# Row scaling beside items 4 to 11, and raw weight blocks and background weights in two spare half buffers

## The chip, the cores and the metric

The program runs on one core of a Trainium2 chip. The metric is device time in microseconds (us) of one execution; lower is better. Three executions of the kernel before took 2995.53, 2995.94 and 2998.75 us, a median of 2995.94. The profile is that of a further execution, which took 2992.3 us in all and 2990.3 us from its first instruction to its last.

## The reference

The model is a trunk of two layers over one sequence of 1024 rows with 1024 channels, all in float32. Layer 0 mixes with a gated delta rule, layer 1 with retention; each is followed by a projection, a residual with layer norm, and a gated feed-forward network (FFN) with a short convolution. A conditioning vector gives each layer scales, shifts and gates ("ada").

```
# layer 1's mixer
q, k, v, gate = split(h @ w_in)            # 4 heads; q, k: 256 channels, v, gate: 512 per head
q, k = rope(q), rope(k)
o = chunked retention over 8 chunks of 128 rows (state S per head)
o = layer-norm-like per head (no affine) of o, times silu(gate)
out = o @ w_out
# after each mixer
x = layer_norm(ALPHA * x + (1 + ada_gate) * out) * g + b
```

The gate row "1 + ada_gate" of layer 1's retention is `silu(c) @ ada_w[1][:, 2*1024:3*1024] + ada_b`: a vector times a 1024 x 1024 block. The kernel computes it on VectorE (DVE), a weight row block at a time, in the background of other work.

## The kernel before, in words

Matmuls are float32-accurate: every operand is split into a high and a low part (fp32r), and three matmuls of 128x512 make one product (`mm3`, L110 to L112; `L1138` and `L616` for other callers). TensorE (PE) therefore does almost all of the span. The split of a block is one copy on ScalarE (ACT, L89, the high part) and one subtraction on DVE (L90, the low part).

The instructions are recorded in program order and then ordered by a scheduler which models the time of each; buffers are tiles with a fixed number per tag ("wr": two of 128x1024, "xT": two of 128x512, "auh", "lane" and so on). A tile's load waits until the last reader of the tile before it in the same buffer is done. Loads are issued by SyncE (SP), one queue, in its order; a DMA in front that waits holds up the ones behind it. So the tag of a load sets when it can start.

Places that the change touches:

- **The opening** (to about 70 us) uses the two "xT" buffers for transposed input (L517). After that they are unused for the rest of the kernel.
- **Layer 1's q, k and gate stage** (about 1430 to 1790 us): a Strassen-Winograd scheme over 16 items, `strassen(..., direct=True, beside=scale_rows)`. Items 0 and 1 are done plainly by `side`; items 2 to 15 by `wino(n)`: two raw weight blocks of 128x1024 are loaded (`ua` by L1190, `ub` by L1191, both tag "wr"), sums s1 to s4 of their halves are made on DVE (L1184, `psub`), split (L89, L90), and seven products of twelve matmuls each are made. Items 2, 4, 5, 7, 9, 11, 12 and 14 are q or k blocks: their outputs go through a rotation on DVE (L1614 to L1619, 12 instructions of 128x512), and are stored by GpSimd (POOL) to `qd` (L1620). The others are gate blocks, which end on ACT (L1629).
- **scale_rows(n)** is called by `wino(n)`. Before, it does for each of items 8 to 15 two blocks of 128x512 of the residual rows: SP loads `xg` (L1646), POOL multiplies by the layer norm's gain and adds its bias (L1647, L1648), and POOL stores the block (L1649).
- **The transition** (about 1775 to 1800 us): SP loads `xlo`, the rows from which the other half of the transposed input is made (PE L259); `qk` from `qd` (L1806); and `wr<-in_ret_wv` (L102), the raw weights of v.
- **The core** (about 1790 to 2150 us): a stream `ret_fill` makes v (`ret_v`, L616; its weights go through both "wr" buffers, each then split by ACT L89 into `wh` and by DVE L90 into `wl`), and runs interleaved with the streams `core(h)` of the four heads: state update Sr (DVE L1739, L1741), output, its normalisation `on` (DVE L1761 to L1767), the product with the gate `ot` (L1776).
- **The background weights of the core**: `bg_ada(1, 2, "row")` gives 16 steps. A step loads 128x2x512 `mvw` (L210, tag `bg_tag[0]`, which is "wr" there) and does two DVE instructions (L214 for the first, then L216: `ada = mvw * e + ada`). Eight such instructions make a half of the vector (four steps of L210 each); then PE sums over partitions (L238) and DVE adds it to the row (L239). Two halves are made.

Of the kernel before, what the change touches and what calls it, by code (L numbers as in the profile page):

```python
# [12 lines left out]
ALU = mybir.AluOpType  # L13
AX = mybir.AxisListType

P = 128
D = 1024
S = 1024
KT = D // P
HALF = 512  # L20
# [13 lines left out]
def trunk_kernel(ctx: ExitStack, tc, A):  # L34
# [166 lines left out]
    def bg_ada(i, j, kind):  # L201
        box = {}

        def unit(nh, kp):
            if kp == 0:
                box["a"] = tl("ada", [P, HALF])
            a = box["a"]
            wr = tl(bg_tag[0], [P, 2, HALF], name="mvw")
            c0 = j * D + nh * HALF
            sp.dma_start(wr, A["ada_w"][i, kp * 256:(kp + 1) * 256, c0:c0 + HALF].rearrange("(a p) n -> p a n", p=P))  # L210
            for kk in range(2):
                k = kp * 2 + kk
                if k == 0:
                    dve.tensor_scalar(a, wr[:, 0], e[:, 0:1], None, ALU.mult)  # L214
                else:
                    dve.scalar_tensor_tensor(a, wr[:, kk], e[:, k:k + 1], a, ALU.mult, ALU.add)  # L216
            if kp < KT // 2 - 1:
                return
            if kind == "col":
                if nh == 0:  # L220
                    vecs[i, j] = ct(f"v{i}{j}", [P, KT])
                gs = slice(4 * nh, 4 * nh + 4)
                v, b = vecs[i, j][:, gs], bias_cols(i, j)[:, gs]
                tp, pt = bg_ps[0](), tl("sm2", [P, 4], name="cs")
                for g in range(4):
                    pe.transpose(tp[:, g * P:(g + 1) * P], a[:, g * P:(g + 1) * P], ident)
                for g in range(4):
                    act.activation(a[:, g * P:(g + 1) * P], tp[:, g * P:(g + 1) * P], AF.Copy, accum_out=pt[:, g:g + 1])
                if j in (1, 2, 4):
                    dve.scalar_tensor_tensor(v, pt, 1.0, b, ALU.add, ALU.add)  # L230
                else:
                    dve.tensor_add(v, pt, b)
            else:
                if nh == 0:
                    rows[i, j] = row_load(A["ada_b"][i:i + 1, j * D:(j + 1) * D], ("x", i))
                g = rows[i, j][nh]
                pt = bg_ps[0]()
                pe.matmul(pt, ones, a, start=True, stop=True)  # L238
                dve.scalar_tensor_tensor(g, pt, 1.0, g, ALU.add, ALU.add)  # L239

        for nh in range(2):
            for kp in range(KT // 2):
                bg.append(lambda nh=nh, kp=kp: unit(nh, kp))
# [888 lines left out]
    def strassen(hT0, xts, scale, shift, items, tags=("hTb", "hTb", "qkv", "qkv", "aux"), direct=False, beside=None):  # L1132
# [53 lines left out]

        def wino(n, sink):
            ua, ub = items[n][:2]
            wa, wb = tl("wr", [P, D]), tl("wr", [P, D])
            sp.dma_start(wa, ua)  # L1190
            anchor["i"] = sp.dma_start(wb, ub)  # L1191
            if beside:
                beside(n)
            a11, a12, a21, a22 = wa[:, hs(0)], wa[:, hs(1)], wb[:, hs(0)], wb[:, hs(1)]
            def copy_of(X, tag="cv"):
                t = tl(tag, [P, 516] if tag == "cv" else [P, HALF], name="pc")[:, 0:HALF]
                act.activation(t, X, AF.Copy)  # L1197
                return t

            X = prod(a11, "11")  # L1200
            p1 = copy_of(X)
            s1 = psub(a21, a22, ALU.add)
            sink(0, prod(a12, "21"), p1)
            s2 = psub(s1, a11)
            Z = prod(s1, "T1")
            z5 = copy_of(Z)
            s4 = psub(a12, s2)
            prod(s2, "T2", X)
            u2 = copy_of(X)
            s3 = psub(a11, a21)  # L1210
            prod(s4, "22", Z)
            sink(1, Z, u2)
            bg_step()
            prod(s3, "T3", X)
            u3 = copy_of(X, "t2")
            sink(3, X, z5)
            sink(2, prod(a22, "T4"), u3)
            bg_step()
# [416 lines left out]
    gb = []  # L1635

    def scale_rows(n):
        for u in range(2 * (n - 8), 2 * (n - 8) + 2) if n >= 8 else ():
            c, rs = u // 8, slice(u % 8 * P, u % 8 * P + P)
            if u % 8 == 0:  # L1640
                gb[:] = [tl("auh", [P, HALF], name="gb") for _ in range(2)]
                for t, nm in zip(gb, ("ln_g", "ln_b")):
                    sp.dma_start(t, A[nm][1:2, hs(c)].to_broadcast([P, HALF]))
            x = tl("auh", [P, HALF], name="xg")
            with after("i"):
                sp.dma_start(x, xs[1][rs, hs(c)])  # L1646
            pool.tensor_tensor(x, x, gb[0], ALU.mult)  # L1647
            pool.tensor_tensor(x, x, gb[1], ALU.add)  # L1648
            pool.dma_start(xg[0][rs, hs(c)], x)  # L1649
# [175 lines left out]
            yield r  # L1825

    mix = []
    events["core", -1] = clk[0]
    free["qkv"] = 20
    run([(0.0, ret_fill())] + [(-1.0, core(h)) for h in range(RH)])  # L1830
    layer_tail(1, mix, None, xs[1], xs[2], A["out"], None, True)


# [100 lines left out]
```

## Time and profile before

| what | value |
|---|---|
| median of three executions | 2995.94 us (2995.53 to 2998.75) |
| the profiled execution | 2992.3 us, span 2990.3 us |
| mean granted TensorE clock | 0.980 |
| PE busy | 2827.8 us, 95% of the span |
| DVE busy | 2191.9 us, 73% |
| ACT busy | 1347.4 us, 45% |
| POOL busy | 604.6 us, 20% |
| L216 (`ada<-mvw,e,ada`), all of the kernel | 140 instructions, 107.1 us, 27.2 us of DVE's idle time before them |

How to read it. PE is busy for 95% of the span, so time can be won or lost only where PE stands idle, and where its granted clock is below 1: after an idle time of some microseconds PE runs at half clock for a while. DVE is not the engine with the most work, yet an instruction of PE often waits for one on DVE, and DVE runs its instructions in a fixed order: one that waits for a DMA holds up all behind it. "[2.40 <-DVE wb L90]" behind a row means that the engine had been idle for 2.40 us, and that the wait ended with an instruction of DVE at line 90 which writes a tile named wb.

### The profile page before, as it was taken

What the parts mean: (1) busy time and instruction counts of PE and PEld (TensorE: products, weight loads), DVE (VectorE), ACT (ScalarE), POOL (GpSimd) and SP (SyncE); (2) the same over time, 40 slices, a digit from 0 to 9 for tenths busy, and PEclk for the clock granted to TensorE, in tenths of its full rate; (3) what the DMA queues carried; (4) which work ended last, traced back from release to release, by engine and by line L of the source; (5) the groups of instructions that cost most, each with busy time, mean ns of one, the idle gap of its engine ahead of it and who ended that gap; (6) DMA issues with size and microseconds to landing.
All of it is one profiled execution on the core that took longest, in us unless ns stands there. A gap on an engine that the chain in (4) does not pass through costs nothing.

```text
span 2990.3 us, 38893 instructions
## 1 busy us (share of the span) xinstructions
PE 2827.8 (95%) x13638; PEld 2308.4 (77%) x13638; DVE 2191.9 (73%) x3877; ACT 1347.4 (45%) x2513; POOL 604.6 (20%) x629
## 2 busy tenths in 40 slices
PE   8889998999999999999999989989999899999996
PEld 7768877887778888877787777767778688888785
DVE  5785687545588888997677665656687787778888
ACT  4655555434544444536443333212345544445444
POOL 0411221133011111520002330232201011112603
PEclk9999999999999999999999999999999999999998
DMA  7222221344344444864424453556573333335652
GB/s 273 86 77 72 96 89 64 117 159 137 110 141 162 155 151 147 311 204 135 154 79 145 157 210 119 170 169 183 169 248 125 127 134 106 106 106 200 242 179 106
DMA packets 235379, 442.35 MB, mean 148 GB/s; under 512 B 22192, under 2 KB 75696, under 8 KB 235184
## 3 DMA queue, kind: packets, MB, share of 16 engines
q1 hardware_dynamic: 205024, 387.96, 38.9%
q10 hardware_dynamic: 25152, 34.61, 3.2%
q0 software_dynamic: 5008, 17.30, 1.5%
q8 instruction: 107, 1.75, 0.2%
q14 instruction: 88, 0.72, 0.1%
HBM read 331.26 MB, written 108.53 MB: 147 GB/s over the span
## 4 chain that ended last, share of the span: by engine, by line
PE 68%; DVE 13%; issue 8%; DMA 6%; ACT 4%; POOL 2%; SPq 0%; POOLq 0%; ACTq 0%; DVEq 0%
PE acc L616 15%; PE acc L1412 11%; PE acc L1138 8%; PE acc L110 5%; PE acc L111 4%; PE acc L112 4%; PE sc L616 4%; PE sc L1138 3%; PE sc L1412 3%; PE mm L616 2%; PE sc L111 2%; PE sc L110 2%; PE sc L112 2%; DMA mvw<-in_ada_w 1%; DVE qkv L435 1%
## 5 line engine op out<-in xcount | busy, mean ns | idle before, releaser
L1412 PE MATMUL acc<-bb,ab 128*128 128x512 f32 x1800 | 427.7, 392 | 3.7 <-DVE bb L90 1.5
L1412 PEld LDWEIGHTS acc<-bb,ab 128*128 128x128 f32 x1800 | 337.3, 188 | 78.2 <-DVE bb L90 3.9
L616 PE MATMUL acc<-hT,wh 128*128 128x512 f32 x960 | 301.2, 395 | 0.0
L1548 POOL TENSOR_TENSOR o<-o 128x512 f32<-128x512 f32 x88 | 118.3, 1354 | 719.5 <-DVE o L1541 684.7
L1138 PE MATMUL acc<-T,wb 128*128 128x512 f32 x840 | 209.4, 400 | 12.6 <-DVE wb L90 12.6
L616 PEld LDWEIGHTS acc<-hT,wh 128*128 128x128 f32 x960 | 183.4, 191 | 33.8
L616 PE MATMUL acc<-hT,wl 128*128 128x512 f32 x480 | 203.5, 424 | 0.2 <-ACT sg L1064 0.2
L89 ACT ACTIVATE ab<-ar 128x512 fp32r<-128x512 f32 x210 | 129.4, 624 | 158.7 <-PE acc L1412 85.6
L1138 PEld LDWEIGHTS acc<-T,wb 128*128 128x128 f32 x840 | 161.2, 193 | 50.6 <-DVE wb L90 16.9
L90 DVE TENSOR_TENSOR ab<-ar,ab 128x512 fp32r<-128x512 f32 x210 | 172.9, 830 | 30.1 <-ACT ab L89 29.7
L90 DVE TENSOR_TENSOR wb<-wr,wb 128x512 fp32r<-128x512 f32 x162 | 114.2, 710 | 86.8 <-ACT wb L89 86.5
L90 DVE TENSOR_TENSOR wl<-wr,wh 128x1024 fp32r<-128x1024 f32 x85 | 104.2, 1225 | 97.3 <-ACT wh L89 97.3
L89 ACT ACTIVATE wh<-wr 128x1024 fp32r<-128x1024 f32 x101 | 106.8, 1058 | 129.9 <-PE acc L616 61.5
L90 DVE TENSOR_TENSOR wb<-mm,wb 128x512 fp32r<-128x512 f32 x216 | 145.1, 685 | 21.1 <-ACT wb L89 19.1
L1197 ACT ACTIVATE pc<-acc 128x512 f32<-128x512 f32 x143 | 84.6, 592 | 160.9 <-PE acc L1138 108.2
L89 ACT ACTIVATE wb<-mm 128x512 fp32r<-128x512 f32 x216 | 122.4, 593 | 76.5 <-DVE mm L1184 76.2
L89 ACT ACTIVATE wb<-wr 128x512 fp32r<-128x512 f32 x162 | 98.9, 626 | 98.8 <-DMA wr<-in_ffn_up 49.5
L616 PE MATMUL acc<-wh,hT 128*128 128x512 f32 x384 | 137.1, 420 | 2.5 <-DVE vv L90 1.6
L1527 DVE SCALAR_TENSOR_TENSOR o<-g,vc,o 128x512 f32<-128x512 f32 (+2 forms) x176 | 135.3, 787 | 0.9 <-ACT o L1522 0.2
L435 DVE SCALAR_TENSOR_TENSOR qkv<-raw,vc,qkv 128x512 f32<-128x512 f32 x144 | 114.8, 801 | 26.8 <-ACT qkv L433 25.5
L216 DVE SCALAR_TENSOR_TENSOR ada<-mvw,e,ada 128x512 f32<-128x512 f32 x140 | 107.1, 765 | 27.2 <-DMA mvw<-in_ada_w 27.1
L110 PE MATMUL acc<-T,wb 128*128 128x512 f32 x292 | 116.7, 400 | 9.9 <-DVE wb L90 9.4
(620 smaller groups left out, 7079.8 us busy)
## 6 DMA issues: line engine op xcount, KB each, us to landing
wr<-in_ffn_up SPq DMA_DIRECT2D x96, 512.0 KB, 4.4
mvw<-in_ada_w SPq DMA_DIRECT2D x80, 512.0 KB, 4.4
ad<-o SPq DMA_DIRECT2D x154, 256.0 KB, 2.3
ar<-ad SPq DMA_DIRECT2D x154, 256.0 KB, 4.0
Br<-in_ffn_down SPq DMA_DIRECT2D x66, 256.0 KB, 3.8
wr<-in_ret_wv SPq DMA_DIRECT2D x32, 512.0 KB, 3.9
ar<-od SPq DMA_DIRECT2D x56, 256.0 KB, 5.2
xs<-xt ACTq DMA_DIRECT2D x24, 512.0 KB, 3.1
```

What stands on the lines that cost most here:

```text
L89: act.activation(dst_h, src, AF.Copy)
L90: eng.tensor_tensor(dst_l, src, dst_h, ALU.subtract)
L110: mm(acc, wl[:, k], hl[0], start=first, stop=False)
L111: mm(acc, wh[:, k], hl[1], start=False, stop=False)
L112: mm(acc, wh[:, k], hl[0], start=False, stop=last)
L216: dve.scalar_tensor_tensor(a, wr[:, kk], e[:, k:k + 1], a, ALU.mult, ALU.add)
L435: dve.scalar_tensor_tensor(oh, raw[:, 3 - j:515 - j], w[:, 3 - j:4 - j], oh, ALU.mult, ALU.add)
L616: pq(pe.matmul(out, lhsT, rhs, start=start, stop=stop, **kw), cost)
L1138: return pe.matmul(*a, skip_group_check=True, **kw)
L1412: mm_ = (lambda *a, p=p, onto=onto, **kw: (mm if p < 2 else pe.matmul)(*a, skip_group_check=onto, **kw))
L1527: dve.scalar_tensor_tensor(tv, gv[:, c0 - j:c1 - j], w[:, 2 - j:3 - j], tv, ALU.mult, ALU.add)
L1548: pool.tensor_tensor(o[d], o[x], o[y], op)
```

## The change

Three things are changed.

1. `scale_rows` does its two blocks beside items 4 to 11 and not beside items 8 to 15. The work is the same.
2. In the q, k and gate stage the raw weight blocks of `wino` are numbered m = 2n (`ua`) and 2n + 1 (`ub`). Every third one (m = 6, 9, ... 30, nine blocks) is loaded as two halves of 128x512 into the two "xT" buffers; the others go through the two "wr" buffers as before. So three raw blocks can be held and not two.
3. During the core `bg_tag` is "xT": a step of the background weights is loaded as two halves of 128x512 into the two "xT" buffers, by two DMAs of 256 KB in place of one of 512 KB. Both "wr" buffers are left to the weights of v.

The numbers of instructions on PE, ACT, DVE and POOL stay as they are; SP issues 17 DMAs more (1184 before, 1201 now).

```diff
@@ bg_ada
-            wr = tl(bg_tag[0], [P, 2, HALF], name="mvw")
             c0 = j * D + nh * HALF
-            sp.dma_start(wr, A["ada_w"][i, kp * 256:(kp + 1) * 256, c0:c0 + HALF].rearrange("(a p) n -> p a n", p=P))
+            src = A["ada_w"][i, kp * 256:(kp + 1) * 256, c0:c0 + HALF].rearrange("(a p) n -> p a n", p=P)
+            if bg_tag[0] == "xT":
+                wr = [tl("xT", [P, HALF], name="mvw") for _ in range(2)]
+                for a2 in range(2):
+                    sp.dma_start(wr[a2], src[:, a2])
+            else:
+                wt = tl(bg_tag[0], [P, 2, HALF], name="mvw")
+                sp.dma_start(wt, src)
+                wr = [wt[:, 0], wt[:, 1]]
             for kk in range(2):
                 k = kp * 2 + kk
                 if k == 0:
-                    dve.tensor_scalar(a, wr[:, 0], e[:, 0:1], None, ALU.mult)
+                    dve.tensor_scalar(a, wr[0], e[:, 0:1], None, ALU.mult)
                 else:
-                    dve.scalar_tensor_tensor(a, wr[:, kk], e[:, k:k + 1], a, ALU.mult, ALU.add)
+                    dve.scalar_tensor_tensor(a, wr[kk], e[:, k:k + 1], a, ALU.mult, ALU.add)
@@ wino
-            wa, wb = tl("wr", [P, D]), tl("wr", [P, D])
-            sp.dma_start(wa, ua)
-            anchor["i"] = sp.dma_start(wb, ub)
+            raws = []
+            for m, u in ((2 * n, ua), (2 * n + 1, ub)):
+                if direct and m % 3 == 0:
+                    raws += [tl("xT", [P, HALF], name="wr") for _ in range(2)]
+                    for h2 in range(2):
+                        anchor["i"] = sp.dma_start(raws[-2 + h2], u[:, hs(h2)])
+                else:
+                    w = tl("wr", [P, D])
+                    anchor["i"] = sp.dma_start(w, u)
+                    raws += [w[:, hs(0)], w[:, hs(1)]]
             if beside:
                 beside(n)
-            a11, a12, a21, a22 = wa[:, hs(0)], wa[:, hs(1)], wb[:, hs(0)], wb[:, hs(1)]
+            a11, a12, a21, a22 = raws
@@ scale_rows
-        for u in range(2 * (n - 8), 2 * (n - 8) + 2) if n >= 8 else ():
+        for u in range(2 * (n - 4), 2 * (n - 4) + 2) if 4 <= n < 12 else ():
@@ the core
+    bg_tag[0] = "xT"
     events["core", -1] = clk[0]
     free["qkv"] = 20
     run([(0.0, ret_fill())] + [(-1.0, core(h)) for h in range(RH)])
+    bg_tag[0] = "wr"
```

The scheduler's order moves with it. Line numbers of the changed kernel are higher: L1184 becomes L1191, L1190 and L1191 become L1201 (half blocks) and L1204, L210 becomes L213 (half blocks), L214 and L216 become L221 and L223, lines from 1214 on become higher by 14.

**SP at the end of the q, k and gate stage.** Before, in a row (`xg` are the rows to be scaled, `qk` the rotated blocks, `xlo` the rows to be transposed, `wr<-in_ret_wv` v's weights):

```order
L1646 DMA xg<-xs_67 128x512 x2
L1190 DMA wr<-in_ret_wg 128x1024
L1191 DMA wr<-in_ret_wg 128x1024
L1646 DMA xg<-xs_67 128x512 x2
L1806 DMA qk<-qd 128x512 x2
L1665 DMA xlo<-xs_67 128x512 x2
L1806 DMA qk<-qd 128x512 x10
L102 DMA wr<-in_ret_wv 128x1024
L1665 DMA xlo<-xs_67 128x512 x2
L102 DMA wr<-in_ret_wv 128x1024
```

Now, at the same place (`mvw` are the background weights):

```order
L1204 DMA wr<-in_ret_wg 128x1024
L102 DMA wr<-in_ret_wv 128x1024
L1679 DMA xlo<-xs_67 128x512 x2
L1820 DMA qk<-qd 128x512 x2
L213 DMA mvw<-in_ada_w 128x512
L1820 DMA qk<-qd 128x512 x7
L1679 DMA xlo<-xs_67 128x512 x2
L102 DMA wr<-in_ret_wv 128x1024
L1785 DMA gt<-gd 128x4x128
L1820 DMA qk<-qd 128x512 x3
L213 DMA mvw<-in_ada_w 128x512 x2
L102 DMA wr<-in_ret_wv 128x1024 x2
```

The `xg` loads are gone from here, v's first weights stand ahead of the `qk` loads, four of the `qk` loads stand earlier still, and the first background weights are loaded here and not in the middle of the core.

**DVE at the transition.** Before, from the last sums of item 15 (`hT` and `wl` are splits for v):

```order
L1129 TENSOR_TENSOR pc<-sc,pc 128x512 x2
L90 TENSOR_TENSOR wl<-wr,wh 128x1024
L90 TENSOR_TENSOR hT<-t_15335,hT 128x512
L90 TENSOR_TENSOR hT<-t_15345,hT 128x512
L90 TENSOR_TENSOR wl<-wr,wh 128x1024
L90 TENSOR_TENSOR hT<-t_15355,hT 128x512
L90 TENSOR_TENSOR hT<-t_15365,hT 128x512
L90 TENSOR_TENSOR wl<-wr,wh 128x1024 x2
```

Now:

```order
L223 SCALAR_TENSOR_TENSOR ada<-mvw,e,ada 128x512
L90 TENSOR_TENSOR hT<-t_15353,hT 128x512
L90 TENSOR_TENSOR hT<-t_15363,hT 128x512
L223 SCALAR_TENSOR_TENSOR ada<-mvw,e,ada 128x512
L90 TENSOR_TENSOR wl<-wr,wh 128x1024
L90 TENSOR_TENSOR hT<-t_15373,hT 128x512
L223 SCALAR_TENSOR_TENSOR ada<-mvw,e,ada 128x512
L90 TENSOR_TENSOR hT<-t_15383,hT 128x512
L223 SCALAR_TENSOR_TENSOR ada<-mvw,e,ada 128x512
L90 TENSOR_TENSOR wl<-wr,wh 128x1024
L223 SCALAR_TENSOR_TENSOR ada<-mvw,e,ada 128x512 x3
L90 TENSOR_TENSOR wl<-wr,wh 128x1024
```

All eight background instructions of the vector's first half now stand here (the first, L221, inside the rotation of item 14), where before they stood in the core between 1960.9 and 2003 us. The last three stand ahead of the split of the fifth weight block of v.

**DVE in the core, at the second half of the background vector.** Before (the first row is the first background instruction, the last `on` is the one whose time the prediction speaks of):

```order
L214 TENSOR_SCALAR ada<-mvw,e 128x512
L1741 SCALAR_TENSOR_TENSOR Sr<-Sr,sc 128x512
L216 SCALAR_TENSOR_TENSOR ada<-mvw,e,ada 128x512
L1741 SCALAR_TENSOR_TENSOR Sr<-Sr,sc 128x512
L1776 TENSOR_TENSOR ot<-mm,gt 128x512
L216 SCALAR_TENSOR_TENSOR ada<-mvw,e,ada 128x512
L1704 SCALAR_TENSOR_TENSOR kz<-mm,vc,kz 128x256
L1706 TENSOR_TENSOR sT<-mm,dx 128x128
L216 SCALAR_TENSOR_TENSOR ada<-mvw,e,ada 128x512
L90 TENSOR_TENSOR sThl<-sT,sThl 128x128
L1761 BN_STATS rst<-sc 128x6
L1763 BN_AGGR mv<-rst 128x2
```

Now, from behind the sT of that piece on:

```order
L223 SCALAR_TENSOR_TENSOR ada<-mvw,e,ada 128x512 x2
L90 TENSOR_TENSOR sThl<-sT,sThl 128x128
L1775 BN_STATS rst<-sc 128x6
L1777 BN_AGGR mv<-rst 128x2
L223 SCALAR_TENSOR_TENSOR ada<-mvw,e,ada 128x512
L1778 TENSOR_SCALAR mv<-mv 128x1
L90 TENSOR_TENSOR wl<-wr,wh 128x1024
L223 SCALAR_TENSOR_TENSOR ada<-mvw,e,ada 128x512
L1781 TENSOR_SCALAR on<-sc,mv 128x512
L1755 SCALAR_TENSOR_TENSOR Sr<-Sr,sc 128x512
L223 SCALAR_TENSOR_TENSOR ada<-mvw,e,ada 128x512
```

Before, four of the eight background instructions stand ahead of the `on` that follows this piece, and four behind it; now six stand ahead of it (the L221 and the first L223 as in the piece before, and the four in this one) and two behind. They are fed by a ring of two half blocks.

## The prediction, made blind

> **What bounds the kernel now.** I read the page's head first, then PE, clock and DMA by stretches of the stage that the change touches, then what PE waited for there.
>
> ```profile
> PE 2827.8 (95%) x13638; PEld 2308.4 (77%) x13638; DVE 2191.9 (73%) x3877; ACT 1347.4 (45%) x2513; POOL 604.6 (20%) x629
> PE 68%; DVE 13%; issue 8%; DMA 6%; ACT 4%; POOL 2%; SPq 0%; POOLq 0%; ACTq 0%; DVEq 0%
> ```
>
> PE is the bound, so only its idle time and its clock can be won. The stretches (columns: busy time and instructions of each engine, granted clock, DMA share, GB/s):
>
> ```profile
> 1440.00:1460.00 20.00, 20.00 (x91) 16.55 (x90) 15.08 (x38) 7.92 (x20) 2.19 (x4) 1.00 0.42 158
> 1660.00:1680.00 20.00, 17.60 (x71) 14.13 (x70) 16.20 (x26) 6.87 (x13) 5.68 (x6) 0.91 0.46 170
> 1720.00:1740.00 20.00, 16.65 (x66) 13.33 (x66) 16.81 (x26) 5.71 (x10) 8.88 (x8) 0.91 0.33 119
> 1780.00:1800.00 20.00, 16.44 (x64) 12.48 (x63) 5.63 (x7) 6.64 (x10) 0.91 (x2) 0.83 0.97 350
> 2000.00:2050.00 50.00, 44.35 (x189) 33.76 (x190) 36.14 (x69) 10.14 (x18) 6.19 (x13) 0.93 0.51 159
> ```
>
> Where nothing waits (1440), PE is busy throughout at full clock. In the others it idles and the clock drops: the missing clock costs 20 x 0.09 = 1.8 us in each of the first two, 20 x 0.17 = 3.4 us at 1780, 50 x 0.07 = 3.5 us at 2000. What PE waited for, by groups of 1427 to 1790 us (last column) and by single rows (in brackets the idle time and who ended it):
>
> ```profile
> L1138 PE MATMUL acc<-T,wb 128*128 128x512 f32 x216 | 55.6, 409 | 7.5 <-DVE wb L90 7.5
> L1138 PE MATMUL sc<-T,wb 128*128 128x512 f32 x120 | 29.4, 394 | 4.0 <-DVE wb L90 4.0
> 1530.70 0.50 PE L1138 MATMUL sc<-T,wb 128*128 128x512 f32 x1 [0.61 <-DVE wb L90]
> 1590.08 0.73 PE L1138 MATMUL sc<-T,wb 128*128 128x512 f32 x2 [1.06 <-DVE wb L90]
> 1670.46 3.86 PE L1138 MATMUL acc<-T,wb 128*128 128x512 f32 x9 [2.40 <-DVE wb L90]
> 1734.22 0.74 PE L1138 MATMUL acc<-T,wb 128*128 128x512 f32 x2 [3.35 <-DVE wb L90]
> 1789.83 0.69 PE L259 MATMUL mm<-cst,xlo 128*128 128x128 f32 x2 [2.70 <-DMA xlo<-xs]
> 1791.34 0.79 PE L616 MATMUL acc<-wh,hT 128*128 128x512 f32 x1 [0.82 <-ACT wh L89]
> 2003.93 1.65 PE L616 MATMUL sc<-vv,sThl 128*128 128x512 f32 x3 [4.96 <-DVE Sr L1739]
> ```
>
> So four places: the rotations (11.5 us idle + 3.6 of clock), the transition (2.70 + 0.82 + 3.4 = 6.9), the core's first background half (4.96 + 3.5, and small gaps), and its second half.
>
> **The rotations: -5 us.** There are eight gaps, one behind each q or k item, since DVE's split of the next block is queued behind the rotation. Two things make them long:
>
> ```profile
> L1616 DVE TENSOR_TENSOR rm<-pc,sinT 128x512 f32<-128x512 f32 x16 | 16.4, 1025 | 0.0
> L1617 DVE TENSOR_TENSOR pc<-pc,cosT 128x512 f32<-128x512 f32 x16 | 14.9, 930 | 0.2
> L1618 DVE TENSOR_TENSOR rm<-rm,pc 128x512 f32<-128x512 f32 x16 | 11.0, 685 | 0.0
> 1658.52 1.78 DVE L1616 TENSOR_TENSOR rm<-pc,sinT 128x512 f32<-128x512 f32 x1
> 1656.76 2.99 POOL L1647 TENSOR_TENSOR xg<-xg,gb 128x512 f32<-128x512 f32 x2 [11.21 <-DMA xg<-xs]
> 1656.04 0.70 DVE L1184 TENSOR_TENSOR mm<-wr 128x512 f32<-128x512 f32 x1 [2.43 <-DMA wr<-in_ret_wg]
> DVE mm L1184 <- DMA wr<-in_ret_wg: 5.9, 5, 2.4
> DVE mm L1184 <- DMA wr<-in_ret_wqk: 1.8, 2, 1.0
> ```
>
> First, the same DVE operation takes 685 ns alone and up to 1.78 us beside POOL's scaling; over the two slowed lines that is 16 x (1025 - 685) + 16 x (930 - 685) ns = 9.4 us. [...] Second, DVE stands 7.7 us (5.9 + 1.8) before a weight block that lands late; 2.43 of it just ahead of the rotation at 1658, whose gap is 2.40. With a third buffer the block's load is issued one block earlier, so I take these waits as gone. The scaling is not: of the eight rotations (items 2, 4, 5, 7, 9, 11, 12, 14) items 9, 11, 12 and 14 are in its range before, and 4, 5, 7, 9 and 11 now. That speaks against the change: one more rotation is exposed. But the worst gap is that of 12, close behind 11, and there the scaling leaves; its twin is 5, close behind 4 (1.06 without scaling). I take 0.6 for 2 and 14, 1.1 for 4, 7, 9, 11 and 12, 2.2 for 5 (between 1.06 and 3.35): 8.9, and one clock drop in two cases, 0.9. That is 15.1 - 9.8, say -5. Bounds: all gaps at 0.61 (-10); the same pairs at the old price in items 4 and 5 and one more exposed gap of 1.2 (+1).
>
> [...] Here a gap of 2.40 already brings the slice to 0.91, one of 2.70 to 0.83: the row decides. [...]
>
> **The transition: -4 us.** PE waits for the second pair of `xlo`, whose buffer is freed by the store of the last rotation:
>
> ```profile
> 1775.06 0.71 POOL L1620 DMA_DIRECT2D qd<-rm  x1 [5.88 <-DVE rm L1618]
> 1783.42 1.24 SPq L1665 DMA_DIRECT2D xlo<-xs  x2
> qd<-rm POOLq DMA_DIRECT2D x16, 512.0 KB, 4.8
> xg<-xs SPq DMA_DIRECT2D x16, 256.0 KB, 5.4
> ```
>
> The store took 8.4 us to free the buffer (1775.06 to 1783.42) against a median of 4.8, with transfers crowded (DMA share 0.97). The scaling's loads and stores leave this place and v's first weights are there earlier; at the median the pair lands about 3.5 us earlier, and eight matmuls of v (8 x 0.23 = 1.8 us) now stand ahead of the transposes. So 2.70 goes, with 0.82 and most of the clock: -5.5 of 6.9.
>
> Against it stands the moved background chain. Its eight DVE instructions use two half buffers, so the load of each waits for the instruction two before it:
>
> ```profile
> mvw<-in_ada_w SPq DMA_DIRECT2D x8, 512.0 KB, 4.5
> gt<-gd SPq DMA_DIRECT2D x9, 256.0 KB, 4.7
> 1812.91 1.23 DVE L90 TENSOR_TENSOR wl<-wr,wh 128x1024 fp32r<-128x1024 f32 x1 [4.21 <-ACT wh L89]
> ```
>
> Half the size lands no sooner (4.7 against 4.5). The second and third load stand behind `qk` and come at about 1790; from there to the eighth are three rounds of 4.5 + 0.75, to about 1806, then `wl` of the fifth block (1.23) at 1807. Before, it ran at 1812.91; with PE some 5 us earlier it is wanted at about 1809. So nothing, up to 3 us late if a round takes longer: I take +1.5. Sum -4; bounds -6.9 and +3. The added waits also hold the `hT` splits that stand among them, which PE needs only with that fifth block. [...]
>
> **The core's first half: -8 us.**
>
> ```profile
> 1990.71 1.54 DVE L216 SCALAR_TENSOR_TENSOR ada<-mvw,e,ada 128x512 f32<-128x512 f32 x2 [5.39 <-DMA mvw<-in_ada_w]
> 2000.72 0.75 DVE L216 SCALAR_TENSOR_TENSOR ada<-mvw,e,ada 128x512 f32<-128x512 f32 x1 [5.78 <-DMA mvw<-in_ada_w]
> 2003.19 1.28 DVE L1739 COPY Sr<-sc 128x512 f32<-128x512 f32 x2
> PE acc L616 <- DVE vv L90: 0.7, 1, 0.7
> PE mm L619 <- DVE on L1767: 0.7, 1, 0.7
> ```
>
> DVE stands 5.78 us before a background block with `wl` and Sr behind it, and PE's 4.96 is the wait for that Sr. These instructions have left, and no `mvw` stands among v's weights on SP. 4.96 + 3.5 of clock + about 1.4 of small gaps = 9.9; I take -8, bounds -4 (clock and half the gap stay) and -10.
>
> **The core's second half: +3 us.** Here six background instructions now stand ahead of one `on`, where four did:
>
> ```profile
> 2033.95 0.75 DVE L216 SCALAR_TENSOR_TENSOR ada<-mvw,e,ada 128x512 f32<-128x512 f32 x1
> 2037.77 0.81 DVE L1767 TENSOR_SCALAR on<-sc,mv 128x512 f32<-128x512 f32 x1
> 2038.08 1.53 PE L616 MATMUL sc<-vv,kz 128*128 128x512 f32 x6
> 2049.64 0.73 PE L616 MATMUL sc<-vv,kz 128*128 128x512 f32 x2 [1.72 <-DVE on L1767]
> ```
>
> The third and fourth come where the trace has 2033.95, each after a load of about 4.5 from a buffer freed at 2030.3 and 2031.5; the fifth and sixth start one round later, at 2038.5 and 2040; `on` ends at about 2042.3 and not 2038.6. PE's six matmuls at 2038.08 write two buffers; the second, after 0.7 us, is the one that `on` frees, so PE stands about 3.5 us from 2038.8, with a clock drop (1.7, as after 2.40), and the gap of 1.72 at 2049.64 is absorbed by the delay: 3.5. I take +3, bounds 0 (loads land in 2 us less) and +6.
>
> The rest (two loads pulled into the opening, where SP waits anyway, and a few rows exchanged in the later projection and FFN): 0, between -2 and +2.
>
> **Sum.** -5 - 4 - 8 + 3 = -14 us. From the profiled 2992.3 that is 2978.3; the median lies 3.6 above that execution, so 2995.9 - 14 = 2982 us.
>
> **Rivals.**
> (a) *The scaling only changes places, and the chain takes back the transition.* Gaps at 4 and 5 cost what those at 9 and 12 did, and the chain's +3 and no freed clock cancel the transition: only -8 + 3 are left: 2991. For it: five exposed rotations against four. Against: the 2.43 us wait is another cause, and it goes.
> (b) *Slower: the ring of two half blocks.* Each background instruction is a DMA round trip standing in DVE's order ahead of `wl` and `on`. If a half lands not in 4.5 but in 8.4 us, as the crowded store at 1775 did, the chain ends at 1790 + 3 x 9.15 + 1.2 = 1818.7, 9.5 late, with 2 of clock; and `on` comes 2 x 3.9 = 8 later than in the sum above, +11 there. 11.5 + 11 against -5 - 5.5 - 8 is +4: 3000. It decides from a landing of about 7.5 us. For it: DMA share 0.97 at the transition. Against: that share holds xg traffic which leaves, and 4.5 in the core.
> (c) *All gaps go*: -10 - 6.9 - 10 and no new stall: 2969. For it: each has a cause that the change touches. Against: the order of DVE in the second half.
> [...]
>
> **How the numbers follow.** The sum's case 0.57 (by itself 2975 to 2989), (a) 0.19, (b) 0.10, (c) 0.09, (d) 0.05. A measurement of this kernel tells about 0.2% (6 us) from no change. Faster than 2990: nearly all of the sum's case, a third of (a), all of (c) and (d): 0.76. Same: 0.16 from (a) and the mild form of (b); slower 0.08 from (b). The range 2970 to 2994 leaves out most of (b) and half of (c), and a little of the rest.
>
> **What would show it.** Right: gaps `<-DVE wb` of 1427 to 1790 sum to 8 to 10 us with none above 2.4 at items 9 and 12; `mm <- DMA wr` near 0; no PE wait for `xlo` above 1; no wait for Sr near 2000; a new gap `<-DVE on` of about 3.5 near 2025 to 2035. Wrong: a PE wait for `wl` some 20 us into the v stage, or a slice with clock below 0.95 there; DVE's slowed L1616 with gaps of 2 to 3 us at items 4 and 5; L223 waiting 5 us or more for several `mvw`.

## The result and the profile after

The changed kernel took 2978.99 us (median of six executions, 2973.88 to 2983.14); the kernel before, in the same comparison, 2995.74 us (six, 2987.61 to 2998.75). The ratio is 0.9947, 95% interval 0.9932 to 0.9962: about 16 us faster. In a second comparison it was 0.9942 (0.9920 to 0.9964). The forecast was 2982 us.

The page's head of the changed kernel, and PE, clock and DMA by stretches (columns as in the prediction; the stretches are moved with the kernel's progress):

```profile
span 2972.1 us, 38933 instructions
PE 2824.1 (95%) x13638; PEld 2305.0 (78%) x13638; DVE 2195.7 (74%) x3877; ACT 1347.1 (45%) x2513; POOL 603.5 (20%) x629
...
1660.00:1680.00 20.00, 19.39 (x86) 15.75 (x85) 16.16 (x26) 6.96 (x13) 3.19 (x6) 1.00 0.42 150
1720.00:1740.00 20.00, 18.94 (x84) 15.37 (x83) 15.26 (x26) 7.28 (x13) 1.43 (x2) 1.00 0.36 131
1770.00:1790.00 20.00, 20.00 (x95) 16.48 (x96) 10.60 (x16) 8.22 (x13) 2.69 (x4) 1.00 0.99 349
1980.00:2030.00 50.00, 48.14 (x215) 37.36 (x214) 36.27 (x69) 10.45 (x18) 8.84 (x15) 0.97 0.52 160
```

The two slices of the rotations and the transition are back at full clock, and at the transition PE does not idle at all, though transfers are as crowded as they were (DMA share 0.99, before 0.97). What PE still waited for, by groups of the q, k and gate stage and by single rows:

```profile
L1145 PE MATMUL acc<-T,wb 128*128 128x512 f32 x216 | 52.4, 391 | 2.9 <-DVE wb L90 2.9
L1145 PE MATMUL sc<-T,wb 128*128 128x512 f32 x115 | 28.2, 394 | 4.5 <-DVE wb L90 4.5
...
1593.61 0.73 PE L1145 MATMUL sc<-T,wb 128*128 128x512 f32 x2 [2.69 <-DVE wb L90]
1671.57 0.50 PE L1145 MATMUL acc<-T,wb 128*128 128x512 f32 x1 [0.61 <-DVE wb L90]
1730.95 0.73 PE L1145 MATMUL acc<-T,wb 128*128 128x512 f32 x2 [1.06 <-DVE wb L90]
2017.99 0.50 PE L623 MATMUL sc<-vv,kz 128*128 128x512 f32 x1 [1.86 <-DVE on L1781]
```

The rotations' gaps fell from 11.5 to 7.4 us. The long ones of items 9 and 12 are 0.61 and 1.06; item 5 has got one of 2.69. The wait for Sr is gone, and a gap of 1.86 in the second half has come.

**Where the time went.** For a sum by place I took each instruction of ACT (the same 2513 in every kernel) and its start in a profile less its start in the profile of before; the change of that shift over a stretch, as the median of the instructions near its two ends, is what the stretch gained (-) or lost (+). Stretches are in the time of the kernel before: rotations 1500 to 1765, transition to 1840, core's first half 1940 to 2010, second half 2010 to 2080, and the rest to the end. The kernels of the other rows are explained below.

| kernel | shift at 1500 | rotations | transition | core, 1st half | core, 2nd half | rest | sum from 1500 on | ratio of medians to before (95%) |
|---|---|---|---|---|---|---|---|---|
| predicted | 0 | -5 | -4 | -8 | +3 | 0 | -14 | 0.9953 |
| the change | +1.9 | -7.2 | -7.1 | -10.6 | +0.4 | +4.2 | -20.1 | 0.9947 (0.9932-0.9962) |
| the change, again | +9.7 | -5.9 | -7.2 | -10.6 | +1.2 | +1.5 | -20.9 | 0.9942 (0.9920-0.9964) |
| scaling alone | +6.2 | -1.8 | -4.6 | -0.8 | +0.4 | -1.5 | -8.3 | 1.0004 (0.9990-1.0018) |
| raw blocks alone | +8.1 | -6.0 | -7.1 | +0.9 | -0.5 | +0.8 | -12.0 | 0.9967 (0.9954-0.9981) |
| background weights alone | +2.3 | +3.0 | 0.0 | -10.7 | -0.4 | -0.9 | -9.0 | 0.9994 (0.9979-1.0009) |
| without the scaling's move | +10.8 | -5.7 | -7.4 | -10.4 | +0.5 | +0.5 | -22.4 | 0.9932 (0.9908-0.9955) |
| without the background weights' part | +7.3 | -5.0 | -7.1 | +1.1 | -1.4 | -1.2 | -13.5 | 0.9965 (0.9950-0.9981) |
| without the raw blocks' part | +7.9 | +1.3 | -2.9 | -10.5 | +1.9 | -0.5 | -10.4 | 0.9985 (0.9970-1.0000) |
| before, without the POOL instructions | +16.1 | -8.4 | -4.5 | +0.3 | -1.1 | -2.0 | -15.7 | one execution |
| scaling leaves item 6 | +17.8 | -8.8 | -7.1 | -10.5 | +1.1 | +0.3 | -24.9 | 0.9945 (0.9927-0.9963) |
| second half in the raw buffers | +5.8 | -5.2 | -7.2 | -10.6 | -1.2 | -1.7 | -26.1 | 0.9924 (0.9901-0.9946) |
| both of these | +4.8 | -8.4 | -7.2 | -10.5 | +1.9 | +0.6 | -23.8 | 0.9920 (0.9902-0.9937) |

How far this can be read: the shift at 1500 us, before anything of the change matters, lies between 0.8 us (the run one head earlier, below, which has no row here) and 17.8 us though DVE's order up to there is the same in all, and the one profile of before was the earliest of all fourteen there. Whole executions therefore differ by several us for reasons that lie outside the change, and sums by place share one reference profile: they exceed the gains by the ratios by up to 9.5 us. Differences between rows of one column are firmer than a row's sum: the two profiles of the change differ by at most 1.3 us in the first four stretches.

### The profile page after: what moved, and what is told of

Same layout as the page of the kernel before. It is cut to its first block, busy times and chain, and to the rows that moved or that the text cites. A ratio compares the mean times of both kernels' runs of the same rounds, so it can differ in the third digit from the quotient of the medians.

```text
span 2972.1 us, 38933 instructions
## 1 busy us (share of the span) xinstructions
PE 2824.1 (95%) x13638; PEld 2305.0 (78%) x13638; DVE 2195.7 (74%) x3877; ACT 1347.1 (45%) x2513; POOL 603.5 (20%) x629
## 3 DMA queue, kind: packets, MB, share of 16 engines
q8 instruction: 107, 1.75, 0.2%
## 4 chain that ended last, share of the span: by engine, by line
PE 63%; DVE 13%; issue 11%; DMA 7%; ACT 4%; POOL 2%; SPq 0%; POOLq 0%; DVEq 0%; ACTq 0%
PE acc L623 15%; PE acc L1426 10%; PE acc L1145 6%; PE acc L110 4%; PE sc L623 4%; PE acc L111 4%; PE acc L112 4%; PE sc L1145 3%; PE sc L1426 3%; PE mm L623 2%; DMA mvw<-in_ada_w 2%; PE sc L111 1%; PE sc L110 1%; PE sc L112 1%; DMA wr<-in_ffn_up 1%
## 5 line engine op out<-in xcount | busy, mean ns | idle before, releaser
L1191 DVE TENSOR_TENSOR mm<-wr 128x512 f32<-128x512 f32 x108 | 80.3, 744 | 72.7 <-DMA wr<-in_ffn_up 46.4
```

## The experiments

**Each of the three parts alone.** The scaling alone is the kernel before with

```diff
-        for u in range(2 * (n - 8), 2 * (n - 8) + 2) if n >= 8 else ():
+        for u in range(2 * (n - 4), 2 * (n - 4) + 2) if 4 <= n < 12 else ():
```

> Only the scaling of rows is moved (items 4 to 11); raw blocks and background weights as before. By the steps of the prediction: rotations -2 us (the gap of 3.35 at item 12 falls to about 1.1 and its clock drop goes; the 2.40 at item 9, which has a late weight block ahead of it, stays), transition -5 to -7 (the 2.70 before the second xlo pair goes, as the scaling's loads and stores have left), core 0 (the 4.96 before Sr stays): about -8, 2988 by the median before. The rival: the transition is mended by v's first weights standing ahead on SP, which needs the raw buffers free, so the scaling alone gains nothing there: about -2.

Measured: ratio 1.0004, no change. By place the rotations gained 1.8 and the transition 4.6. PE's gap at item 5, and the transition's stretch:

```profile
1598.77 0.50 PE L1145 MATMUL sc<-T,wb 128*128 128x512 f32 x1 [3.06 <-DVE wb L90]
...
1778.00:1798.00 20.00, 17.76 (x79) 13.70 (x79) 10.13 (x15) 9.54 (x15) 2.35 (x4) 1.00 0.94 328
```

The gap at item 12 fell from 3.35 to 1.35, as expected, the one at item 9 stayed at 2.40, and item 5 got 3.06. So the long gap only moved from the second of one pair of rotations to the second of the other. The places say -8, the clock of twelve executions +1 with an interval of about 4 us on either side; that they disagree stays open.

The raw blocks alone:

```diff
-            wa, wb = tl("wr", [P, D]), tl("wr", [P, D])
...
+                if direct and m % 3 == 0:
+                    raws += [tl("xT", [P, HALF], name="wr") for _ in range(2)]
...
```

> Only every third raw block goes through the spare half buffers. By the steps of the prediction: the waits of the sums for late weight blocks (7.7 us before) go, the 2.40 gap at item 9 falls below 1.2, the 3.35 at item 12 falls little since the scaling still runs beside it: -3 to -4; transition and core as before. The rival: contention with the scaling makes all of the long gaps, so nothing changes at items 9 and 12: 0.

Measured: 0.9967, about 10 us, three times what the steps gave. The groups of PE, two rows, a rotation's instruction on DVE, the waits for weight blocks, DVE's last wait ahead of item 9's rotation with that rotation's start, and the transition's stretch:

```profile
L1145 PE MATMUL acc<-T,wb 128*128 128x512 f32 x216 | 53.8, 399 | 4.1 <-DVE wb L90 4.1
L1145 PE MATMUL sc<-T,wb 128*128 128x512 f32 x120 | 29.4, 394 | 2.9 <-DVE wb L90 2.9
...
1676.20 0.97 PE L1145 MATMUL acc<-T,wb 128*128 128x512 f32 x3 [0.60 <-DVE wb L90]
1736.79 0.73 PE L1145 MATMUL acc<-T,wb 128*128 128x512 f32 x2 [2.25 <-DVE wb L90]
...
L1630 DVE TENSOR_TENSOR rm<-pc,sinT 128x512 f32<-128x512 f32 x16 | 16.4, 1023 | 0.0
...
DVE mm L1191 <- DMA wr<-in_ret_wqk: 13.9, 6, 3.0
DVE mm L1191 <- DMA wr<-in_ret_wg: 11.6, 6, 2.4
...
1657.92 0.70 DVE L1191 TENSOR_TENSOR mm<-wr 128x512 f32<-128x512 f32 x1 [2.26 <-DMA wr<-in_ret_wg]
...
1663.76 1.77 DVE L1630 TENSOR_TENSOR rm<-pc,sinT 128x512 f32<-128x512 f32 x1
...
1778.00:1798.00 20.00, 20.00 (x98) 16.52 (x97) 9.44 (x13) 9.42 (x14) 2.40 (x3) 1.00 0.94 333
```

Three things at once speak against my steps. The rotation's instruction is as slow as before (1023 ns, before 1025) and the scaling still runs beside it, yet all gaps but one are at their floor of 0.6 to 1.1. The sums wait longer for their blocks (25.5 us in all, before 7.7) and it costs nothing: the scheduler now lets them stand earlier in DVE's order, where DVE has time to wait. Ahead of item 9 the wait of 2.26 us ends 5.8 us before the rotation starts; in the kernel before, the one of 2.43 us ends 2.5 us before it. And the transition's gap is gone with all of the scaling's traffic still there.

The background weights alone, with the half loads of `bg_ada` as in the change:

```diff
+    bg_tag[0] = "xT"
     events["core", -1] = clk[0]
...
+    bg_tag[0] = "wr"
```

> Only the background weights of the core use the spare half buffers. The first half's eight instructions stand in the middle of the q, k and gate stage in this one. By the steps of the prediction: the core's first half -8 to -10 (no wait of 4.96 for Sr, no clock drop near 2001), the second half 0 to +3, the rotations +1 at most (6 us more of DVE work there), transition 0: about -8. The rival (the ring of two half blocks costs as much as it gives): a stall of 3.5 or more in the second half and new gaps at the rotation that holds the eight instructions: 0 or slower.

Measured: 0.9994. By the clock that is no change, as the rival forecast; by place it is -9.0, as the prediction's steps had it; that the two disagree stays open here too. The core's first half gained 10.7, and the rival's second price showed as well, at item 2's rotation, where PE and DVE have:

```profile
1536.14 0.79 PE L1145 MATMUL sc<-T,wb 128*128 128x512 f32 x1 [3.56 <-DVE wb L90]
...
1526.93 0.75 DVE L223 SCALAR_TENSOR_TENSOR ada<-mvw,e,ada 128x512 f32<-128x512 f32 x1 [1.17 <-DMA mvw<-in_ada_w]
```

With the spare buffers free since the opening, the scheduler hoists the background instructions into the rotation of item 2 (0.61 before): 3.56 and a clock drop. In the full change the raw blocks hold these buffers through the stage, so that the same eight instructions come no earlier than its end, where they cost nothing.

**One part undone.** The diffs are those above, reversed, against the full change.

> The change without the move of the scaling (it stays beside items 8 to 15). DVE's order is that of the full change. If the raw blocks' third buffer alone mends rotations and transition, as the run with it alone suggests (gaps of 0.6 but for 2.25 at item 12, no gap before xlo), this one is within 3 us of the full change, 2979 to 2982, with the gap of 2 to 3 us at item 12 and none at item 5. The prediction's step (the scaling's traffic has to leave the transition) gives a gap of some 2.7 us before xlo and a clock drop: 6 to 7 us slower than the full change, 2985 or more.

Measured: 0.9932, the full change 0.9947 and 0.9942. The gap is at item 12 and not at item 5:

```profile
1600.89 0.50 PE L1145 MATMUL sc<-T,wb 128*128 128x512 f32 x1 [1.06 <-DVE wb L90]
1739.33 1.04 PE L1145 MATMUL acc<-T,wb 128*128 128x512 f32 x3 [2.17 <-DVE wb L90]
```

and the transition gained 7.4 without the move. So the scaling's move adds nothing that can be measured to the two other parts, and the transition does not need the scaling's traffic to leave.

> The change without the background weights' part (they stay in the raw buffers). The core's wait of about 5 us for Sr and its clock drop stay near 2000, the rest as in the full change: 10 us slower than the full change, about 2988 if places add up. The rival (the background chain at the transition and in the second half takes back what the core gains): within 3 us of the full change.

Measured: 0.9965, some 5 to 7 us slower than the full change by the ratios, 11.7 by place in the core's first half (+1.1 against -10.6). PE's wait for Sr is there again:

```profile
1999.58 0.80 PE L623 MATMUL sc<-vv,sThl 128*128 128x512 f32 x1 [5.51 <-DVE Sr L1753]
```

> The change without the third raw buffer. The background vector's first half then stands beside items 2 and 3, as in the run with the background weights alone, and costs a gap of 3 to 4 us there; late weight blocks stay, so the gaps at items 9 and 12 stay near 2.4 and 1.3; transition mended by the scaling's move, core -10: about -9 in all, 2986. The prediction's steps give -4 for the transition, -5 for the core with its second half and -2 for the rotations: -11. If instead the scaling's move gains nothing without the third buffer (as its run alone says by the clock): -2, 2993.

Measured: 0.9985, 2991 us by the median, between the forecasts. The transition gained only 2.9, and the rotations lost 1.3. Whether the background weights' part gives less without the third raw buffer is not shown by the clock. Without that buffer it gave 2 us alone (0.9994) and 6 us on top of the scaling (from 1.0004 to 0.9985); with it, 10 us on top of the raw blocks (from 0.9967 to 0.9932) and 5 to 7 us on top of both other parts, with intervals of some 4 us or more on either side of each ratio. What the places show is the loss of 1.3 to 3.0 in the rotations.

**Contention alone.** From the kernel before, the scaling's two POOL instructions are left out:

```diff
-            pool.tensor_tensor(x, x, gb[0], ALU.mult)
-            pool.tensor_tensor(x, x, gb[1], ALU.add)
```

> The kernel before without the scaling's two POOL instructions (the rows are loaded and stored unscaled); loads, stores and the order of all else stay. If contention makes the long gaps, those at items 9 and 12 (2.40 and 3.35) fall to about 1.1 or below, and the rotation's slowed instructions run in 685 ns. If late weight blocks make them, 2.40 at item 9 stays, since the sum still waits 2.4 us for its block. The gap before xlo stays at 2 to 3 us if traffic makes it.

Measured in one execution, whose rows stay unscaled. PE at item 9, the rotation's instruction on DVE, and the sums' wait:

```profile
1684.13 0.73 PE L1145 MATMUL acc<-T,wb 128*128 128x512 f32 x2 [0.61 <-DVE wb L90]
...
L1630 DVE TENSOR_TENSOR rm<-pc,sinT 128x512 f32<-128x512 f32 x16 | 11.0, 686 | 0.0
...
DVE mm L1191 <- DMA wr<-in_ret_wg: 5.7, 5, 1.8
```

Item 9 falls from 2.40 to 0.61 and item 12 from 3.35 to 1.49, with the waits for late gate blocks nearly as they were (5.7 in all, before 5.9; the one ahead of item 9 is 1.79, before 2.43). By place the rotations gain 8.4, near the most that any kernel here reached (8.8). So taking away the contention mends the gap of item 9, and so does the third raw buffer with the contention left: that gap needs both. The kernel before says the same by itself. Its rotations of items 7, 11 and 14 are slowed by POOL like that of item 9; with waits of 0.81 to 0.90 us ahead of them they have gaps of 1.12 to 1.22, and item 9, with 2.43 ahead, has 2.40. Item 12, close behind item 11, needs only the contention: 3.35 with a wait of only 0.38 beside it, and still 2.25 with the third buffer. My reading is that DVE has a slack before PE waits in each rotation. I estimate it at 2.3 to 2.7 us from those four items: the slowing (2.07 us in each) plus the wait, less what the gap has above 0.61. Either delay of item 9 fits into that, and both together do not. The gap before `xlo` is gone in this run as well, though all of the scaling's loads and stores are still there.

**A version that keeps the gain and mends what is left.** First the scaling's items:

```diff
-        for u in range(2 * (n - 4), 2 * (n - 4) + 2) if 4 <= n < 12 else ():
+        for u in range(2 * (3, 4, 5, 7, 8, 9, 10, 11).index(n), 2 * (3, 4, 5, 7, 8, 9, 10, 11).index(n) + 2) if n in (3, 4, 5, 7, 8, 9, 10, 11) else ():
```

> The full change, with the scaling beside items 3, 4, 5, 7, 8, 9, 10 and 11: it leaves item 6, whose rows are scaled during the rotation of item 5, close behind that of item 4. If the scaling during the second of two neighbouring rotations makes the one long gap that is left (2.69 at item 5), that gap falls to about 1.06, all others stay at 0.61: -1.6 us against the full change, and -1.7 more where its clock drop fell. The rival (the late weight block makes it): the gap stays above 2.

```profile
1607.94 0.73 PE L1145 MATMUL sc<-T,wb 128*128 128x512 f32 x2 [1.06 <-DVE wb L90]
```

Exactly the expected 1.06, though a late block still stands ahead of this rotation (a wait of 2.34 us, in the full change 2.08): the gap of item 5 goes with the scaling of item 6. The rotations gain 8.8. By whole executions (0.9945, in the same comparison the full change 0.9942) the two cannot be told apart.

> As skip6, and the background vector's weights are recorded one head earlier (head 1 and not head 2). The ring of two half blocks is the same; if the stall before the normalised output is the ring's (six background instructions ahead of it), it comes again, one head earlier, at the same size of 2 us with a clock drop by chance: within 2 us of skip6. If it was an accident of that place, it goes, and with it a gap of 2 and up to 1.7 of clock: -2 to -4.

Here, on top of the preceding kernel, `if h == 2:` ahead of `bg_ada(1, 2, "row")` is `if h == 1:`. PE's stall came again, one head earlier:

```profile
1936.00 0.50 PE L623 MATMUL sc<-vv,kz 128*128 128x512 f32 x1 [2.13 <-DVE on L1781]
```

So it belongs to the background chain and not to the place. From 1840 to 2080 us this kernel gains 9.5 us by place and the preceding one 9.3, as expected if the stall only moves. The ratio is 0.9930 (0.9913 to 0.9947), by the median 4 us below the preceding one; the intervals overlap.

> The full change again, on the same chip as the two others: 0.993 to 0.996 of the kernel before. By the two readings of the profile: gaps of 0.6 at the rotations but for 2 to 3 us at item 5, none before the second pair of rows to be transposed, one of about 1.9 in the second half. Whether the clock drops behind a gap of that size depends on where it falls among fixed stretches of 3.41 us.

Measured: 0.9942; gaps of 2.75 at item 5, 2.15 in the second half and, unlike the first profile, 2.33 at 2047.95.

The second half of the vector in the raw buffers:

```diff
-            if bg_tag[0] == "xT":
+            if bg_tag[0] == "xT" and nh == 0:
...
-                wt = tl(bg_tag[0], [P, 2, HALF], name="mvw")
+                wt = tl("wr" if bg_tag[0] == "xT" else bg_tag[0], [P, 2, HALF], name="mvw")
```

> The full change, but the second half of the background vector loads its weights as 512 KB blocks into the raw buffers, as before; the first half keeps the spare half buffers. DVE's order in the second half is again that of the kernel before (four background instructions ahead of the normalised output). If the ring of two half blocks makes the stall of 1.9 to 2.4 us there, it goes, and the two later gaps of 1.7 of the kernel before come back: no net gain, within 3 us of the full change. The prediction's step would have the ring cost 3 us more than the raw buffers: 3 us faster than the full change. The rival (v's weights late for want of the raw buffers): a wait for the weights' split and slower by 3 or more.

```profile
2031.80 0.74 PE L623 MATMUL sc<-vv,kz 128*128 128x512 f32 x2 [1.18 <-DVE on L1781]
2042.13 0.72 PE L623 MATMUL sc<-vv,kz 128*128 128x512 f32 x2 [1.05 <-DVE on L1781]
```

In place of the stall of 1.9 to 2.2 there are gaps of 1.18 and 1.05. By place the second half gained 1.2 where the full change lost 0.4 and 1.2, as if the ring of two half blocks cost 1.6 to 2.4 there; the next run, with DVE's order the same, does not repeat it. Ratio 0.9924 (0.9901 to 0.9946).

> Both repairs together: the scaling leaves item 6 (as in skip6), and the second half of the background vector loads into the raw buffers (as in half2_wr). If their places add up: no gap above 1.1 at the rotations, none above 1.3 in the core before 2060, so no clock drop between 1490 and 2060; 3 to 5 us less than the full change in these places, that is 0.991 to 0.993 of the kernel before. If the two cannot be told from the full change by the clock of whole executions: 0.994.

Measured: 0.9920 (0.9902 to 0.9937), 2971.66 us by the median: the lowest of all, and below the kernel before beyond doubt. Rotations -8.4. The second half is +1.9 here, with gaps of 1.64 and 2.12 and a clock drop, where none above 1.3 was expected, against -1.2 in the preceding run with the same order. So executions differ by 3 us at this place, and what the ring costs stays open. Its interval overlaps that of the full change; that it is better than the full change is likely, not shown.

## Why the prediction was right, and where it was not

The sign and size held: 2982 us forecast, 2979 and 2977 measured, and rival (a) (nothing but the core), (b) (slower) and (c) (all gaps, 2969) did not occur. For (d), at 2986, no run shows a ground; what the changed kernel showed is a gap of 1.86 with half clock (0.50) over the 3.41 us behind it. Of the signs that the prediction had named, those for `xlo`, for Sr and for the new gap behind `on` came. The sums' wait near 0 did not (26.0 us), and one sign of being wrong came in half: a gap of 2 to 3 us at item 5, though not at item 4. Step by step:

**Rotations, -5 forecast, -7.2 and -5.9 measured.** Size right (gaps of 8.9 us forecast, 7.4 measured), and the gaps of single items nearly so: 1.06 at item 12 (1.1 forecast), 2.69 at item 5 (2.2). Two statements behind it were wrong. "I take these waits as gone": they rose from 7.7 to 26.0 us:

```profile
DVE mm L1191 <- DMA wr<-in_ret_wqk: 13.8, 7, 3.3
DVE mm L1191 <- DMA wr<-in_ret_wg: 12.2, 6, 3.4
```

What counts is not how long DVE waits for a block but whether it does so close ahead of a rotation. And the count of exposed rotations was off by one item: the rows of item n are loaded behind its weights, so POOL scales them during the rotation of item n - 1. Before, 7, 9, 11, 12 and 14 were exposed, and now 4, 5, 7 and 9: one fewer, not one more (slowed instructions of a rotation start at 1618, 1659, 1700, 1726 and 1763 us before, and at 1560, 1582, 1620 and 1659 now). Skipping item 6 cleared item 5, which shows it.

**Transition, -4 forecast, -7.1 measured.** This step gave two reasons: the scaling's loads and stores leave this place, and v's first weights, with eight matmuls of v, stand ahead of the second transposes. The first is not needed: with the scaling where it was, the transition gained 7.1 (raw blocks alone) and 7.4 (with the background weights). The second holds in all eight kernels with the raw blocks' part, and each of them gained about 7; it holds in none of the others, and these gained 0 to 4.6.

The landings in the traces tell the two apart. Counted from PE's first transposes at this place, the second pair of rows lands after 8.7 us in the kernel before and 8.6 with the background weights alone, and after 5.8 to 6.9 in all other kernels. PE wants it after 6.1, or after 7.8 where the eight matmuls stand ahead. So an earlier landing alone leaves 0 to 0.9 of the wait of 2.70, the matmuls alone would leave about 0.9 (an estimate, 8.7 - 7.8), and both together leave none. What an earlier landing does not mend is PE's wait for the splits of v's first weights, here in the run with the scaling alone (1785 to 1800 us):

```profile
PE acc L623 <- ACT wh L89: 1.1, 1, 1.1
PE acc L623 <- DVE wl L90: 0.5, 1, 0.5
```

The store that frees the buffer took 8.3 and 8.6 us in the two late kernels and 3.8 to 4.4 in the others, but for 6.5 without the scaling's move. With the raw blocks alone it took 4.3, beside the same loads and stores of the scaling, so what slows it stays open. The term of +1.5 for the background chain was nearly 0:

```profile
1802.35 0.75 DVE L223 SCALAR_TENSOR_TENSOR ada<-mvw,e,ada 128x512 f32<-128x512 f32 x1 [2.75 <-DMA mvw<-in_ada_w]
1803.02 1.22 DVE L90 TENSOR_TENSOR wl<-wr,wh 128x1024 fp32r<-128x1024 f32 x1
...
1804.41 0.99 PE L623 MATMUL acc<-wh,hT 128*128 128x512 f32 x2
```

The chain ends at 1803.1 and the split at 1804.2, and PE runs on through 1804 without an idle time: it came just in time. (The pair of matmuls at 1804.41 took 0.99 us where its neighbours took about 0.6, so at most 0.4 us was lost.) Worked out at 1807 and wanted at 1809 in the time of before, that is 1801.5 and 1803.5 here; it was 2.7 later than worked out. The chain's loads issued at 1781 and 1782 took 6.7 and 6.1 us, and those from 1788 on 2.7 to 4.3, where 4.5 had been put in for each.

**Core's first half, -8 forecast, -10.6 measured.** The mechanism is right: the wait for Sr is there in each kernel without this part (5.0 to 5.5 us) and in none with it. Too cautious: it also takes all of the small gaps and the clock drop (in the changed kernel no idle time above 0.6 us and a clock of 1.00 from 1800 to 2015 us).

**Second half, +3 forecast, +0.4 and +1.2 measured.** The mechanism is right: with six background instructions ahead of `on`, PE stalls behind it. The size was off. The stall was worked out at 3.5 with its clock drop of 1.7 extra; it was 1.86 with one, and 2.15 without one. The term that was mis-sized is the landing of a half block. "Half the size lands no sooner (4.7 against 4.5)" took its price from `gt<-gd` in the kernel before, another transfer of the same size. The half blocks themselves, between 2000 and 2060 us of the changed kernel (where `gt` took 3.8):

```profile
mvw<-in_ada_w SPq DMA_DIRECT2D x6, 256.0 KB, 3.1
...
2012.61 0.90 DVE L223 SCALAR_TENSOR_TENSOR ada<-mvw,e,ada 128x512 f32<-128x512 f32 x1 [1.31 <-DMA mvw<-in_ada_w]
2017.13 0.80 DVE L1781 TENSOR_SCALAR on<-sc,mv 128x512 f32<-128x512 f32 x1
```

Their median from 1900 to 2070 us is 3.1 to 3.4 us in every kernel that loads this half through the ring (3.1 in the changed kernel), and 4.4 to 4.6 for whole blocks in all the others (4.5 in the kernel before), among them the two kernels with this half in the raw buffers. So here halving did bring the landing forward, by 1.0 to 1.5 us, where the prediction had put in 4.5 for a half block too. The fourth instruction waits 1.31 for its half block, where a round of 4.5 had been put in, and `on` ends at 2017.93; with the shift of some 23 us at this place that is 2040.9 in the time of before, 1.4 sooner than worked out. The sum also let the delay take up one of the two later gaps of before (1.72 and 1.75). In the first profile it took up both; in the second one a gap of 2.33 stands where the later of the two was. The background vector is made in eight such load steps of two instructions each, not in 16 steps; the sums used the right count.

**The rest, 0 forecast, +4.2 and +1.5 measured.** The kernels' rests lie between -2.0 and +4.2 with no pattern by part; no run tells a cause.

**The sum** fell short by place (-14 against -20 and -21). Each of the four terms was too cautious, by 1 to 3 us, and the rest, put at 0, took some of that back. That it came within 3 to 5 us of the clock's median is therefore in part luck. The profile of before need not be its median execution in every place, which may be why place and clock differ; no run shows it.

## What to carry to other kernels

Before giving a gap to one of two causes, ask how much slack stands before it: where an engine has some 2.5 us of it (the estimate for the rotations) and each of two delays takes 2 to 2.5, removing either removes the gap, and the second remedy is worth nothing (here the scaling's move). Here a spare buffer was worth more for where it let the scheduler put the waiting instructions than for an earlier transfer (with the raw blocks alone the sums waited 25.5 us for their blocks, before 7.7, and the ratio was 0.9967): look at what the new order waits for, and where. A buffer that becomes free early can also let background work be hoisted into a place without slack (here a gap of 3.56 at item 2, before 0.61), so check where it lands. And the price of a transfer is best taken from the same transfer: here 4.7 us of another load of the same size stood in for what took 3.1.

## What the hardware showed that I had not expected

In the profiles of the changed kernel and of the kernel before, the clock drop goes by fixed stretches of 3.41 us, not by the length of a gap. In each of the two the starts of the half-clock stretches lie on one grid of 3.41 us (counted from the program's first instruction, it begins at 1.17 us in the changed kernel and at 1.25 before), and the drop goes with PE's idle time within one stretch of it. Stretches on the grid of the changed kernel (PE's busy time, clock, DMA share, GB/s), then of the kernel before (all engines):

```profile
1588.38:1591.79 3.41, 2.53 (x12) 1.00 0.37 137
1591.79:1595.20 3.41, 1.59 (x7) 1.00 0.34 130
1595.20:1598.61 3.41, 3.41 (x17) 1.00 0.73 255
2015.05:2018.46 3.41, 1.55 (x7) 1.00 0.85 234
2018.46:2021.87 3.41, 3.41 (x15) 0.50 0.78 271
```

```profile
1666.96:1670.37 3.41, 1.10 (x5) 0.56 (x3) 3.41 (x7) 1.56 (x4) 0.27 (x1) 1.00 0.00 0
1670.37:1673.78 3.41, 3.32 (x8) 2.65 (x9) 3.34 (x7) 1.10 (x2) 1.17 (x2) 0.50 0.60 231
```

The gap of 2.69 at 1593 falls across two stretches, 0.88 in one and 1.82 in the other, and costs no clock. The shorter one of 1.86 at 2018 lies within one, and the next stretch runs at half clock, which costs 1.7 us (half of 3.41). Over these two profiles, from 1300 to 2900 us, all 13 stretches at full clock with at least 1.86 us idle were followed by one at half clock, and none of the 907 with at most 1.82 was. So my "a gap of 2.40 already brings the slice to 0.91, one of 2.70 to 0.83: the row decides" read one throw of a die as a rule. My estimate from these figures: a gap below 1.8 us alone costs none, one above 3.7 (twice 1.86) fills a stretch enough wherever it falls, and one between costs by chance.

The other is the spread of the first half: 0 to 17.8 us of shift at 1500 us between profiles, from layer 0, where DVE's order is the same. It is as large as the effect, and it is why parts of a change of this size are better told apart by place than by the span.
